# The low parts of three of seven weight operands: from a VectorE subtraction to a ScalarE copy and an accumulating DMA

## The chip, the cores and the metric

The kernel runs on one core of one Trainium2 chip. The metric is the device time of one execution in microseconds. TensorE multiplies, VectorE (DVE) and ScalarE (ACT) do elementwise work, GpSimd (POOL) does some sums, masks and reductions, and SyncE (SP) issues nearly all DMAs. Each engine runs its own instructions in order; semaphores tie them together.

## The reference

Two layers over 1024 tokens of 1024 features, in float32. Layer 0 mixes by forgetting attention (8 heads of 128), layer 1 by chunkwise retention (4 heads, keys of 256, values of 512, chunks of 64). Each mixer is followed by a SwiGLU block of inner width 2816. Every block reads an RMS-normed input and adds its result to the residual stream; a last RMS norm ends it.

```python
def swiglu(h, w_in, w_out):
    gu = h @ w_in
    return (jax.nn.silu(gu[..., :D_FF]) * gu[..., D_FF:]) @ w_out

for i in range(DEPTH):
    h = rmsnorm(x, norm_mix[i])
    j = i // N_MIXERS
    if i % N_MIXERS == 0:
        x = x + forgetting_attention(h, fox_w_in[j], fox_b_f[j], fox_w_out[j])
    else:
        x = x + retention(h, ret_w_in[j], ret_w_out[j])
    h = rmsnorm(x, norm_ffn[i])
    x = x + swiglu(h, ffn_w_in[i], ffn_w_out[i])
return rmsnorm(x, final_norm)
```

## The kernel before

**Products in three passes.** TensorE multiplies float32r operands, which keep fewer bits than float32. Each operand is therefore held as the sum of a high part, the operand rounded to float32r, and a low part, the rest. A product takes three matmuls: high by high, high by low, low by high. `split` (line 97) makes the two parts: a ScalarE copy rounds (line 98), a VectorE subtraction makes the rest (line 99). A weight's parts are called wh and wl, an activation's parts b.

**Seven products for eight.** From the attention's output on, most weight products go by a Strassen-Winograd scheme. A pair of column tiles is cut into four blocks of 128 x 512: A11, A12, A21, A22. Seven weight operands are made of them: A11, A12 and A22 are blocks as they come from memory; S1, S2, S3 and S4 are sums and differences that VectorE makes (lines 588, 589, 606, 611). `Blocks` loads a pair as two tiles `st` of 512 KB through SP (line 577) and splits each operand on demand (`get`). `Products` runs one operand through 12 matmuls of 128x512: for four feature tiles, lines 638 (wh by high), 639 (wh by low) and 640 (wl by high). So a pair takes 84 matmuls. `pair_T` uses it for SwiGLU inputs and the retention's queries, keys and gates; `pair_acc` for the pairs of the SwiGLU outputs; `pair_N` does the same by tokens for the retention's values. There are 84 such pairs of blocks: 44 of SwiGLU inputs, 16 of SwiGLU outputs, 16 of queries, keys and gates, 8 of values.

**Buffers.** The parts of weights come from the pool `wp`: six buffers for wh and six for wl. The seventh operand can be split only when the first has left TensorE. The copy of p (line 699) has to take A11's product out of its bank before A12's is added to it.

**What sets the order.** The kernel is written in program order; a scheduler of the framework then puts each engine's instructions in the order they keep on the chip, so operands of neighbouring pairs interleave on TensorE. The order is fixed when the program is built.

**Early operands.** The first pair of three phases has A11 and S2 split ahead of time by `early`, with the plain split.

Of the kernel before, what the change touches and what calls it, by code (L numbers as in the profile page):

```python
# [12 lines left out]
AF = mybir.ActivationFunctionType  # L13
ALU = mybir.AluOpType
# [23 lines left out]
def trunk(ctx, tc, nc, d, out):  # L38
# [22 lines left out]

# [1 line left out]
    bpa = ctx.enter_context(tc.tile_pool(name="bpa", bufs=32))  # L63
    wp = ctx.enter_context(tc.tile_pool(name="wp", bufs=6))
    mp = ctx.enter_context(tc.tile_pool(name="mp", bufs=1, space=PSUM))
    banks = [0]
# [44 lines left out]

# [1 line left out]
    class Norm:  # L113
# [69 lines left out]

    # =================== forgetting attention ===================
    with ExitStack() as fs:
# [11 lines left out]
        norm = Norm(0, fp, "acc", "mx")  # L197
# [217 lines left out]
        reloads = []  # L415
        # the keys of the first two heads, a pass over the features as they come
        ks, pss = [], {}
# [27 lines left out]
        for h in range(FOX_HEADS):  # L445
            if h > 0:
                kk, qq = k1 if h == 1 else k_head(h), q_head(h)
                if h % 2 == 0:
                    vs, _ = v_pair(h // 2, rc)
            if h == FOX_HEADS - 2:  # L450
                os_ = [reload(i) for i in range(FOX_HEADS - 2)]
            if h == FOX_HEADS - 1:
# [1 line left out]
                wo, ops = [], {}  # L454
                for n, b in TILES[:3]:
                    if b == 0:
                        wo.append(wtile(d["fox_o"][n][:, :7 * P], 7))
                    ops[n, b] = mm_fox()
                    mm_u(ops[n, b], wo[n][:6], os_, b, last=False)
            attend(h, kk, qq, vs, dk, rks)  # L460
        os_ += last_o

        # the tiles so far with all heads but the last; the first of them leave the banks
        part = {}
# [15 lines left out]

    # =================== Strassen-Winograd products ===================
    # C = A B with A = W^T in 2 x 2 blocks (two column tiles, even and odd k tiles) and
    # B in 2 x 2 blocks (even and odd k tiles, two token halves): seven products.
    bpb = ctx.enter_context(tc.tile_pool(name="bpb", bufs=24))
# [10 lines left out]

    # where the sums of a phase are kept
    NAMES = ("B11", "T2", "T1", "T3", "B21", "B22", "T4")
# [40 lines left out]
    class Stored:  # L538
        """The sums of a group of four pairs of feature tiles, kept in memory, split at their first use."""

# [23 lines left out]
    def wsplit(src):  # L564
        hi, lo = wh_wl()
        split(hi, lo, src)
        return hi, lo

    class Blocks:
        """The four blocks of a pair of column tiles and their sums, split on demand."""  # L570

        def __init__(self, src):
            self.s1, self.ready = None, {}
            sts = []
            for i in range(2):
                st = sp.tile([P, 1024], F32, tag="st", name=nm("st"), bufs=5)
                nc.sync.dma_start(st, src[:, i * 1024:(i + 1) * 1024])
                sts.append(st)
            self.a11, self.a12 = sts[0][:, 0:512], sts[0][:, 512:1024]
            self.a21, self.a22 = sts[1][:, 0:512], sts[1][:, 512:1024]  # L580
# [15 lines left out]
        def get(self, n):  # L596
            if n in self.ready:
                return self.ready[n]
            if n == "A11":
                return wsplit(self.a11)  # L600
            if n == "S2":
                return wsplit(self.s2)
            if n == "S1":
                return wsplit(self.s1)
            if n == "S3":
                nc.vector.tensor_tensor(self.a21, self.a11, self.a21, op=ALU.subtract)
                return wsplit(self.a21)
            if n == "A12":
                return wsplit(self.a12)
            if n == "S4":  # L610
                nc.vector.tensor_tensor(self.s2, self.a12, self.s2, op=ALU.subtract)
                return wsplit(self.s2)
            return wsplit(self.a22)

# [3 lines left out]
    class Products:  # L618
        """The seven products of one pair of 128-column tiles, feature-major."""

# [21 lines left out]
    def pair_acc(src, X, y, first):  # L642
        """Adds the products of one pair to the sums y over the groups of feature tiles."""
        prod = Products(src, X)
        banks = prod.banks
        if first:
            y.update({n: yu(n) for n in ("11", "12", "21", "22")}, p=qu("p"))

        def add(n, bk):
            nc.vector.tensor_tensor(y[n], banks[bk], y[n], op=ALU.add)  # L650

        def put(n, bk):
            nc.scalar.copy(y[n], banks[bk]) if first else add(n, bk)  # L653

        prod(0)
        put("p", "a")
        prod(1)
        put("12", "b")
        prod(2)
        prod(3)  # L660
        put("22", "b")
        add("22", "c")
        prod(4)
        put("11", "a")
        prod(5)
        add("12", "c")
        prod(6)
        put("21", "b")

    def paired_out(wsrc, stored, scale_rows, xold):  # L670
        """x + (scaled) act @ W over the groups of eight feature tiles whose sums are in memory."""
        ys = [{} for _ in range(4)]
        out = [[None, None] for _ in range(KT)]
        for g, X in enumerate(stored):
            for n in range(4):
                y = ys[n]
                pair_acc(wsrc[g, n], X, y, g == 0)
                if g < len(stored) - 1:
                    continue
                for q in ("12", "21", "22"):  # L680
                    nc.vector.tensor_tensor(y[q], y[q], y["p"], op=ALU.add)
                for i in range(2):
                    for h in range(2):
                        u = y[f"{i + 1}{h + 1}"]
                        if scale_rows:
                            nc.vector.tensor_tensor(u, u, R[:, HALF[h]], op=ALU.mult)
                        xo = sp.tile([P, H], F32, tag="xo", name=nm("xo"), bufs=2)
                        nc.sync.dma_start(xo, xold[2 * n + i][:, HALF[h]])
                        nc.vector.tensor_tensor(u, u, xo, op=ALU.add)
                        out[2 * n + i][h] = u  # L690
        return out

    def pair_T(src, X):
        """Feature-major C11, C12, C21, C22 of one pair of 128-column tiles."""
        prod = Products(src, X)
# [20 lines left out]
    def pair_N(srcs, X):  # L716
        """Token-major C11, C12, C21, C22 of one pair of 256-column tiles, as two tiles of two token blocks."""
        ws = [Blocks(s) for s in srcs]
# [58 lines left out]
    def load_units(pool, src, gate=None):  # L777
        """A feature tile over all tokens from memory, split in two, by token halves."""
        r = []
# [10 lines left out]
    def out_proj(wsrc, y, acts, xnew, gi, nextw, pools):  # L790
        """y + act @ W: returns the operands of the next phase and its norm."""
        norm = Norm(gi, sp, "sc", "sacc", 4)
# [17 lines left out]

    # =================== SwiGLU ===================
    def ffn(i, X, nrm, xold, xnew, last, nw, pools):
# [60 lines left out]

# [1 line left out]
    norm = Norm(1, sp, "sc", "sacc", 4)  # L875
# [34 lines left out]

    # =================== retention ===================
    qd = [[dp.tile([P, S], F32, tag=f"qd{k}", name=f"qd{k}") for k in range(2 * h, 2 * h + 2)] for h in range(RET_HEADS)]
# [81 lines left out]
    def load_k(h):  # L994
        """Keys by feature, split, and the first half of them times kappa by token, split."""
        ks, kf = [], []
# [23 lines left out]
    def state(kt, vv):  # L1020
        """Sum over the first half of the tokens of key times value, by key feature."""
        r = []
# [14 lines left out]
    heads = {}  # L1037
# [131 lines left out]
def _alt(w, i):  # L1169
    """Every other column tile."""  # L1170
    k, n = w.shape
    return w.reshape(k, n // 256, 2, P)[:, :, i].reshape(k, n // 2)


def _quad(u, v, js):
    """A pair of column tiles as four blocks: the first over even and over odd k tiles, then the second."""
    r = [w.reshape(KT // 2, 2, P, -1)[list(js)].transpose(2, 1, 0, 3).reshape(P, 2, -1) for w in (u, v)]
    return np.ascontiguousarray(np.concatenate(r, axis=1).reshape(P, -1))
# [75 lines left out]
```

## Time and profile before

| | |
|---|---|
| time, median of 3 runs | 2627.21 us (2626.6 to 2629.64) |
| span of the profiled execution | 2626.0 us |
| TensorE, matmuls | 2600.0 us, 99%, 12808 instructions |
| VectorE | 1960.2 us, 75% |
| ScalarE | 1155.9 us, 44% |
| POOL | 167.6 us, 6% |
| DMA | 312.11 MB, mean 119 GB/s |

The profiled execution's own time is its span, 2626.0 us; the fastest of the three runs is 0.6 us above it. Matmuls overlap: one lasts about 0.39 us and the next starts 0.23 us after it, so TensorE's time in a stretch is read from how many matmuls start there. Rows of line 638 to 640 are the seven products, rows of 106 to 108 plain products, rows of 737 to 739 the products by tokens.

In time order the program is: the attention to about 500 us, inputs of the first SwiGLU to about 900, its output to about 1165, the retention's projections to about 1610, the retention and its output to about 1960, the second SwiGLU to the end.

### The profile page before, as it was taken

The page shows a single profiled execution, that of the slowest core. Times are in us where ns is not written, and L with a number is a line of the kernel's source. Part 1 is how long each engine was busy: PE and PEld are TensorE (multiplying, and loading weights), DVE is VectorE, ACT ScalarE, POOL GpSimd, SP SyncE. Part 2 cuts the span into 40 slices and gives each one's busy share as a digit, 9 for nine tenths or more (in the row PEclk, how much of TensorE's full clock was granted, in tenths as well). Part 3 has the DMA queues.
Part 4 walks back from the last instruction along what each step waited for, and adds up shares of the span by engine and source line. Part 5 has one row for each costly group of instructions (what it writes and reads, how often), then busy time and mean ns, then how long its engine had stood idle before and what let it go on. Part 6 is the DMA issues. An engine that isn't in the chain of part 4 may idle for free.

```text
span 2626.0 us, 35148 instructions
## 1 busy us (share of the span) xinstructions
PE 2600.0 (99%) x12808; PEld 2179.9 (83%) x12808; DVE 1960.2 (75%) x3367; ACT 1155.9 (44%) x2168; POOL 167.6 (6%) x147
## 2 busy tenths in 40 slices
PE   9999999999999999999999999999999999999998
PEld 8878887888888878889898989898888888887888
DVE  6798888877767778987667676885567776768795
ACT  6566666533233444453333425662353233335533
POOL 0143322000000000001000010000000000000000
PEclk9999999999999999999999999999999999999999
DMA  3111143332332345533332325655522332325441
GB/s 129 44 57 65 49 145 119 122 106 95 109 104 97 109 152 180 167 107 117 104 113 96 113 101 160 189 196 192 190 85 85 104 111 86 109 84 183 156 158 65
DMA packets 137694, 312.11 MB, mean 119 GB/s; under 512 B 15665, under 2 KB 28721, under 8 KB 137521
## 3 DMA queue, kind: packets, MB, share of 16 engines
q1 hardware_dynamic: 136800, 309.33, 35.1%
q8 instruction: 100, 1.64, 0.3%
q14 instruction: 74, 0.60, 0.1%
q10 hardware_dynamic: 720, 0.55, 0.1%
HBM read 217.54 MB, written 92.27 MB: 118 GB/s over the span
## 4 chain that ended last, share of the span: by engine, by line
PE 89%; DMA 4%; DVE 3%; issue 2%; ACT 1%; POOL 0%; SPq 0%; DVEq 0%; POOLq 0%; ACTq 0%
PE mm L638 17%; PE mm L640 17%; PE mm L639 17%; PE mm L106 7%; PE mm L107 7%; PE mm L108 7%; PE mm L738 2%; PE mm L739 2%; PE mm L737 2%; DMA st<-vd 1%; DMA st<-ac_T 1%; PE mm L256 1%; PE mm L258 1%; PE mm L257 1%; DVE b L99 1%
## 5 line engine op out<-in xcount | busy, mean ns | idle before, releaser
L639 PE MATMUL mm<-b,wh 128*128 128x512 f32 x2128 | 836.8, 394 | 0.0
L638 PE MATMUL mm<-b,wh 128*128 128x512 f32 x2128 | 832.9, 395 | 3.2 <-ACT 22_4397_22190 L653 1.8
L640 PE MATMUL mm<-b,wl 128*128 128x512 f32 x2128 | 819.5, 394 | 0.1
L98 ACT CAST wh<-st 128x512 fp32r<-128x512 f32 (+1 forms) x449 | 275.2, 616 | 578.4 <-PE mm L639 409.4
L638 PEld LDWEIGHTS mm<-b,wh 128*128 128x128 f32 x2128 | 400.3, 188 | 97.8 <-ACT 22_4397_22190 L653 2.2
L640 PEld LDWEIGHTS mm<-b,wl 128*128 128x128 f32 x2128 | 399.8, 188 | 94.1 <-DVE wl L99 0.9
L639 PEld LDWEIGHTS mm<-b,wh 128*128 128x128 f32 x2128 | 400.0, 188 | 91.9 <-DVE b L99 0.2
L99 DVE TENSOR_TENSOR wl<-st,wh 128x512 fp32r<-128x512 f32 (+1 forms) x449 | 311.5, 697 | 55.8 <-ACT wh L98 51.8
L98 ACT CAST wh<-s 128x512 fp32r<-128x512 f32 x252 | 156.0, 621 | 413.3 <-PE mm L639 356.8
L106 PE MATMUL mm<-b,wh 128*128 128x512 f32 x736 | 289.7, 397 | 8.4 <-ACT b L126 5.7
L107 PE MATMUL mm<-b,wh 128*128 128x512 f32 x736 | 290.0, 395 | 1.4 <-DVE b L99 1.4
L108 PE MATMUL mm<-b,wl 128*128 128x512 f32 x736 | 289.9, 395 | 0.0
L99 DVE TENSOR_TENSOR wl<-s,wh 128x512 fp32r<-128x512 f32 x252 | 182.6, 727 | 41.4 <-ACT wh L98 39.7
L106 PEld LDWEIGHTS mm<-b,wh 128*128 128x128 f32 x736 | 138.9, 189 | 40.5 <-ACT b L126 6.5
L107 PEld LDWEIGHTS mm<-b,wh 128*128 128x128 f32 x736 | 138.8, 189 | 32.0 <-DVE b L99 1.8
L108 PEld LDWEIGHTS mm<-b,wl 128*128 128x128 f32 x736 | 138.7, 188 | 31.5
L98 ACT CAST b<-st 128x512 fp32r<-128x512 f32 (+1 forms) x216 | 125.1, 612 | 81.7 <-DMA st<-ac_T 30.0
L99 DVE TENSOR_TENSOR b<-st,b 128x512 fp32r<-128x512 f32 (+1 forms) x216 | 140.0, 674 | 27.9 <-ACT b L98 22.5
L711 DVE TENSOR_TENSOR u<-mm,u 128x512 f32<-128x512 f32 x60 | 41.4, 689 | 116.1 <-PE mm L640 115.9
L738 PE MATMUL mm<-wl,b 128*128 128x256 f32 x448 | 126.0, 281 | 0.0
L739 PE MATMUL mm<-wh,b 128*128 128x256 f32 x448 | 125.9, 281 | 0.0
L737 PE MATMUL mm<-wh,b 128*128 128x256 f32 x448 | 125.8, 281 | 0.0
(514 smaller groups left out, 3965.2 us busy)
## 6 DMA issues: line engine op xcount, KB each, us to landing
st<-ffn_in SPq DMA_DIRECT2D x88, 512.0 KB, 3.5
st<-ffn_out_pairs SPq DMA_DIRECT2D x32, 512.0 KB, 5.4
st<-ac_T SPq DMA_DIRECT2D x32, 512.0 KB, 4.6
ac_T<-t SPq DMA_DIRECT2D x48, 256.0 KB, 2.4
st<-ac_B SPq DMA_DIRECT2D x24, 512.0 KB, 4.6
st<-fox_qk SPq DMA_DIRECT2D x32, 256.0 KB, 2.7
xo<-xd SPq DMA_DIRECT2D x32, 256.0 KB, 3.1
ac_B<-p SPq DMA_DIRECT2D x32, 256.0 KB, 3.1
```

The costliest lines, as they stand in the source:

```text
L98: nc.scalar.copy(hi, src)
L99: return nc.vector.tensor_tensor(lo, src, hi.bitcast(F32), op=ALU.subtract)
L106: nc.tensor.matmul(ps, wh, xh, start=(first and k == 0), stop=False)
L107: nc.tensor.matmul(ps, wh, xl, start=False, stop=False)
L108: nc.tensor.matmul(ps, wl, xh, start=False, stop=(last and k == n - 1))
L638: nc.tensor.matmul(ps, hi[:, js], th, start=f, stop=False, skip_group_check=not new)
L639: nc.tensor.matmul(ps, hi[:, js], tl, start=False, stop=False, skip_group_check=not new)
L640: nc.tensor.matmul(ps, lo[:, js], th, start=False, stop=(j == 3), skip_group_check=not new)
L711: nc.vector.tensor_tensor(u2, banks["c"], u2, op=ALU.add)
L737: nc.tensor.matmul(o, th[:, tk], hi[:, js], start=f, stop=False, skip_group_check=sk)
L738: nc.tensor.matmul(o, th[:, tk], lo[:, js], start=False, stop=False, skip_group_check=sk)
L739: nc.tensor.matmul(o, tl[:, tk], hi[:, js], start=False, stop=(j == 3), skip_group_check=sk)
```

## The change

For A11, A12 and A22, apart from the early A11s, a new function `wsplit_added` takes the place of `wsplit`. The high part is a ScalarE copy as before. The low part begins as a second ScalarE copy with a scale of -1, which rounds to the same float32r value with the other sign. Then a DMA that POOL issues adds the block, read from memory again, to it. VectorE has no part in it. `Blocks` keeps the source in memory for that. The new lines move later line numbers by 9: lines 638 to 640 become 647 to 649, line 699 becomes 708, lines 820 and 822 become 829 and 831, lines 932 and 933 become 941 and 942.

```diff
+    def wsplit_added(src, mem):
+
+
+        hi, lo = wh_wl()
+        nc.scalar.copy(hi, src)
+        nc.scalar.activation(lo, src, AF.Copy, scale=-1.0)
+        nc.gpsimd.dma_start(lo, mem, accum_op=ALU.add)
+        return hi, lo
+
...
         def __init__(self, src):
-            self.s1, self.ready = None, {}
+            self.s1, self.ready, self.src = None, {}, src
...
             if n == "A11":
-                return wsplit(self.a11)
+                return wsplit_added(self.a11, self.src[:, 0:512])
...
             if n == "A12":
-                return wsplit(self.a12)
+                return wsplit_added(self.a12, self.src[:, 512:1024])
...
-            return wsplit(self.a22)
+            return wsplit_added(self.a22, self.src[:, 1536:2048])
```

**ScalarE at an A12 of the retention's keys, before.** The first row is the cast of A12's high part, the second the copy of p, then come two SiLUs of the gates and the casts of S4 and A22. The low part is a row of VectorE.

```order
L98 CAST wh_12194<-st_12110 128x512
L699 COPY p_2451_12131<-mm_12118 128x512
L960 ACTIVATE u_2438_12043<-u_2438_12043 128x512
L960 ACTIVATE c_2439_12045<-c_2439_12045 128x512
L98 CAST wh_12211<-s_2453_12134 128x512
L98 CAST wh_12228<-st_12112 128x512
```

The same place now:

```order
L573 CAST wh_12301<-st_12216 128x512
L708 COPY p_2451_12238<-mm_12225 128x512
L574 ACTIVATE wl_12302<-st_12216 128x512
L969 ACTIVATE u_2438_12147<-u_2438_12147 128x512
L969 ACTIVATE c_2439_12149<-c_2439_12149 128x512
L98 CAST wh_12319<-s_2453_12241 128x512
L573 CAST wh_12336<-st_12218 128x512
L574 ACTIVATE wl_12337<-st_12218 128x512
```

The second copy, wl_12302, stands behind the copy of p.

**TensorE at the same A12, now.** The last matmul that reads the S4 operand before it (wh_12169, wl_12170), whose buffers this A12 takes over, has 18 rows between it and the first row of this A12, the third below.

```order
L648 MATMUL mm_12267<-b_10965,wh_12263 128x512
L649 MATMUL mm_12267<-b_10964,wl_12264 128x512
L647 MATMUL mm_12225<-b_10974,wh_12301 128x512
L648 MATMUL mm_12225<-b_10975,wh_12301 128x512
L649 MATMUL mm_12225<-b_10974,wl_12302 128x512
L647 MATMUL mm_12225<-b_10978,wh_12301 128x512
```

The third A12 matmul is the first that reads the low part, so 20 matmuls stand between the release of the buffers and it. Before, it was 22: 20 rows stood between the release and A12's first row, since two more matmuls of the pair ahead came in between.

**ScalarE at a pair of the first SwiGLU's inputs, now.** The rows go from S3's cast through A12, S4 and A22 to the next pair's A11.

```order
L98 CAST wh_6511<-st_6448 128x512
L829 ACTIVATE u_1307_6369<-u_1307_6369 128x512
L573 CAST wh_6531<-st_6446 128x512
L98 CAST wh_6549<-s_1325_6471 128x512
L574 ACTIVATE wl_6532<-st_6446 128x512
L573 CAST wh_6566<-st_6448 128x512
L831 ACTIVATE u_1301_6333<-u_1301_6333 128x512
L708 COPY p_1323_6468<-mm_6455 128x512
L574 ACTIVATE wl_6567<-st_6448 128x512
L573 CAST wh_6594<-st_6590 128x512
L574 ACTIVATE wl_6595<-st_6590 128x512
```

Here the second copy of A12 (wl_6532) stands behind the cast of S4 (wh_6549). Before, the same stretch held the casts alone, one to an operand.

**POOL in the retention's projections, now.** The sums of rotated keys and queries (lines 941 and 942) and the accumulating DMAs share POOL's queue.

```order
L942 TENSOR_TENSOR m_2474_12365<-m_2474_12365,c_2464_12299 128x512
L941 TENSOR_TENSOR m_2471_12354<-m_2471_12354,u_2463_12297 128x512
L942 TENSOR_TENSOR m_2472_12355<-m_2472_12355,p_2451_12238 128x512
L575 DMA wl_12611<-ret_qk 128x512
L575 DMA wl_12646<-ret_qk 128x512
L575 DMA wl_12693<-ret_v 128x512
L575 DMA wl_12698<-ret_v 128x512
```

Before, this queue held the sums alone.

## The prediction

> **What bounds the kernel now.** I read the page's busy shares first, then TensorE by stretch, then who waits for whom.
>
> ```profile
> span 2626.0 us, 35148 instructions
> PE 2600.0 (99%) x12808; PEld 2179.9 (83%) x12808; DVE 1960.2 (75%) x3367; ACT 1155.9 (44%) x2168; POOL 167.6 (6%) x147
> ```
>
> TensorE is busy in 2600 of 2626 us. A busy PE need not be a full one, so the stretches come next (columns: PE, PEld, DVE, ACT, POOL busy with their instructions, granted clock, DMA share, GB/s).
>
> ```profile
> 500.00:900.00 400.00, 400.00 (x1741) 325.01 (x1740) 288.40 (x474) 129.43 (x219) 0.00 (x0) 1.00 0.28 95
> 1000.00:1090.00 90.00, 89.84 (x387) 72.29 (x386) 83.21 (x139) 35.35 (x64) 0.00 (x0) 1.00 0.50 162
> 1165.00:1610.00 445.00, 445.00 (x2589) 391.21 (x2587) 312.61 (x478) 161.33 (x351) 50.30 (x32) 1.00 0.33 109
> ```
>
> The first SwiGLU's input products issue 1741 matmuls in 400 us, 0.23 us each, at full clock. Its output pairs (1000:1090) keep that pitch with VectorE at 92% (83.21 of 90). So VectorE is well filled, yet TensorE hardly waits for it:
>
> ```profile
> PE mm L106 <- ACT b L126: 5.7, 2, 5.5
> ...
> PE rw L165 <- DVE rs_d L153: 1.6, 1, 1.6
> PE cs L159 <- DVE acc L139: 1.5, 1, 1.5
> PE mm L107 <- DVE b L99: 1.4, 1, 1.4
> ...
> PE mm L638 <- DVE 12_1832_9061 L650: 0.2, 1, 0.2
> ...
> ACT wh L98 <- PE mm L639: 766.2, 395, 4.6
> ```
>
> Columns: total us, times, longest. In the seven-product code TensorE's one wait for VectorE is 0.2 us. The last row matters more: ScalarE waits for TensorE 395 times, for a weight buffer. Six operands fit the ring, and the split of the next starts when the oldest leaves. What counts is therefore the time from that release to TensorE's first use of the low part.
>
> **What is removed.** 249 low-part subtractions leave VectorE (84 pairs of tiles, three operands each, less three early A11s):
>
> ```profile
> L99 DVE TENSOR_TENSOR wl<-st,wh 128x512 fp32r<-128x512 f32 x433 | 303.4, 704 | 55.7 <-ACT wh L98 51.8 <-PE mm L108 1.6
> L98 ACT CAST wh<-st 128x512 fp32r<-128x512 f32 x433 | 267.8, 620 | 573.5 <-PE mm L639 409.4 <-PE mm L107 77.3 <-issue 33.9
> L822 ACT ACTIVATE u<-u 128x512 f32<-128x512 f32 x44 | 27.8, 633 | 3.1 <-DVE u L821 3.1
> L699 ACT COPY p<-mm 128x512 f32<-128x512 f32 x60 | 34.8, 579 | 0.0
> L932 POOL TENSOR_TENSOR m<-m,u 128x512 f32<-128x512 f32 x8 | 13.9, 1738 | 0.0
> ```
>
> 249 x 0.704 = 175 us of VectorE. In time they are worth what TensorE waits for VectorE: 0.2 us here, 4.7 us with the other three rows, which lie at norms. I take -2 us, ends 0 and -5.
>
> **What is added on ScalarE.** 249 scaled copies, priced by the 633 ns ACTIVATE: 158 us. They fit, since ScalarE has 129 of 400 us busy in the first stretch and TensorE's pitch covers them; their delay to the low part is counted below. Without that cover they would cost 158 us.
>
> **What is added on the queues.** 249 accumulating transfers of 256 KB, issued by POOL after the second copy. Nothing like that is in this trace: the queue list has hardware-issued queues and instruction fetches alone. The nearest rows (KB each, median us from issue to landing):
>
> ```profile
> q1 hardware_dynamic: 136800, 309.33, 35.1%
> q10 hardware_dynamic: 720, 0.55, 0.1%
> st<-fox_v SPq DMA_DIRECT2D x12, 256.0 KB, 2.5
> x<-xT SPq DMA_DIRECT2D x16, 256.0 KB, 5.3
> st<-ret_v SPq DMA_DIRECT2D x16, 512.0 KB, 3.4
> st<-ret_qk SPq DMA_DIRECT2D x16, 512.0 KB, 4.3
> st<-ffn_out_pairs SPq DMA_DIRECT2D x32, 512.0 KB, 5.4
> ```
>
> Call D the time from the end of the second copy until TensorE may use the sum. The low end is the fastest plain 256 KB load, 2.5 us. The high end is the slowest, 5.3, plus POOL's longest simple instruction, 1.7: 7.0. An accumulation has to take in the block and the tile, 512 KB, so the nearest rows are 512 KB loads of ordinary stretches (3.4 and 4.3), plus about 1 us on POOL: **D = 4.75**, also the middle of the ends. The spread of single transfers I take as half the width of the 256 KB rows, 1.4 us either way. The traffic, 65 MB on top of 309 MB that take 35.1%, adds 7% as plain transfers and some 15% with both reads; shares of 28 to 50% leave room, so it costs nothing but D.
>
> A rule of the Trainium skill gives another D: "DMA: Bandwidth & Descriptors", section "Anatomy of one DMA — SWDGE (gpsimd) path", fits a fixed 2 us plus the bytes at 436 GB/s, an estimate of 2.6 us here, or 3.2 with the bytes counted twice. By that the sum below would be near 7 us or 20 us instead of 57. No row of this trace shows such a transfer.
>
> **Where D decides.** From the order I counted the matmuls that stand between the last use of the reused buffer and the first use of the new low part. A22 always has 62 or more. A12 has few:
>
> - 13 to 20 matmuls: 15 places (13; 15 and 17 and 18 twice each; 20 eight times), of them 6 in the output pairs, 7 in the retention's keys, queries and gates, 2 in the SwiGLU inputs;
> - 24 to 29: 9 places (24, 28, three of 27, four of 29);
> - 30 to 37: 46 places, 38 of them in the SwiGLU inputs, and there every second A11 belongs with them (19 places of 62 matmuls, but behind four other ScalarE instructions). With one or two of the A11s that have 38, some 66.
>
> What ScalarE does meanwhile, at one A12 of before (columns: start, us):
>
> ```profile
> 1251.47 0.62 ACT L98 CAST wh<-st 128x512 fp32r<-128x512 f32 x1 [0.92 <-PE mm L639]
> 1252.00 0.58 ACT L699 COPY p<-mm 128x512 f32<-128x512 f32 x1
> 1252.13 0.69 DVE L99 TENSOR_TENSOR wl<-st,wh 128x512 fp32r<-128x512 f32 x1 [1.03 <-ACT wh L98]
> 1254.05 0.40 PE L640 MATMUL mm<-b,wl 128*128 128x512 f32 x1
> 1254.28 0.40 PE L638 MATMUL mm<-b,wh 128*128 128x512 f32 x1
> ```
>
> VectorE ran beside ScalarE's copy of p, and the low part was there 1.35 us after the cast began. Now the second copy stands behind the copy of p: instructions start 0.53 us apart, so it ends 0.53 + 0.53 + 0.63 = 1.7 us after the cast began, and D follows. A matmul ends 0.17 us after the next one starts (0.40 against 0.23), and the weights load 0.19 us ahead:
>
> ```profile
> L640 PEld LDWEIGHTS mm<-b,wl 128*128 128x128 f32 x2128 | 399.8, 188 | 94.1 <-DVE wl L99 0.9
> ```
>
> So n matmuls leave n x 0.23 - 2.1 us for D.
>
> - 15 places: 0.9, 1.35, 1.8, 2.0 and 2.5 us, mean 2.1. Each is short by 4.75 - 2.1: 15 x 2.65 = 40 us.
> - 9 places: mean 4.2, short by 0.55: 5 us.
> - 66 places. An A12 with 32 matmuls leaves 5.3 us. One with 34 waits on ScalarE behind S4's cast, whose buffers come free 7 matmuls later: 7.8 - 1.6 - 0.17 - 1.16 - 0.19 = 4.7. The A11 has 36 matmuls from that release to its low part and five ScalarE instructions: 8.3 - 0.17 - 2.75 - 0.19 = 5.2. Mean 5.05, 0.3 above D; with a spread of 1.4 either way the mean shortfall is 1.1 x 1.1 / (2 x 2.8) = 0.22: 14 us.
>
> A late low part stops TensorE, whose queue is in order; nothing behind it runs, and all later releases slide by as much. Sum: 40 + 5 + 14 - 2 = **+57 us**, 2626 + 57 = 2683; the median of the runs shown, 2627.2, is 1.2 above this span, so **2684**. At D = 2.5 only seven of the 15 are short, by 6 us: +4. At D = 7 it is 74 + 25 + 129 = +228, less 2.
>
> POOL's own queue adds a wait: in the retention a transfer stands behind four sums of rotated keys (up to 1.7 us each, the POOL row above). Those are A12s with 30 matmuls or more; I leave them in the spread. The moved pieces (ten matmuls of the next S2 ahead of the next A11; loads one place apart on SP) are work that was there before: no cost.
>
> **Rivals.**
>
> 1. *The transfer is hidden* (11%, not slower than the resolution). Place: the 15 A12s. If D is 2.4 us or less, the eight with 20 matmuls are in time, the other seven cost 5 us and VectorE's relief takes some back: 2627 to 2630. For it: the 2.5 us row. Against it: every 512 KB row is 3.4 us or more, and POOL comes on top.
> 2. *Relief wins* (5%). VectorE at 92% in the output pairs loses 48 subtractions; if that ends unseen waits, the gain is at most TensorE's time not busy, 26 us, of which the waits named for VectorE are 5: 2617 to 2621. Against it: only 0.2 us of these lies there.
> 3. *POOL is held up* (13%). If preparing the transfer waits for VectorE, busy 72 to 92% in 0.7 us pieces, three such waits put D at 7: 2626 + 226 + 1 = 2853. It decides from D = 5.05 on, where the 66 places begin to pay in full, 66 us for each further us. For it: VectorE is rarely idle. Against it: no row shows POOL held up by VectorE.
>
> The skill's "SBUF — State Buffer", "Who interferes with whom", has the rule behind the third: two-port VectorE operations shut GpSimd out while it writes descriptors, tensor_tensor is inferred not to. The rows here that are moved or stay are nearly all TENSOR_TENSOR, so by that rule D stays small; no run here shows it yet.
>
> **How the numbers follow.** Forecast, D between 2.7 and 6.3: 71%; its own range, 2634 to 2800. A run of this kernel tells a difference from about 0.2%, 5 us. Faster is rival 2, 5%; within 0.2% is rival 1, 11%, and one point of the forecast's low edge; slower is the rest, 83%. The range 2632 to 2820 leaves out rivals 1 and 2 and the upper part of rival 3.
>
> **What would show it.** TensorE waits named on the low part's DMA, at matmuls of line 649 after A12, total 50 to 70 us, most in the output pairs and the retention, 0 to 1 us per two pairs in the SwiGLU inputs; VectorE busy near 1785 us, ScalarE near 1315; a POOL queue of 249 x 256 KB with 3.5 to 5 us to landing. If landing is under 2.5 us, or no such waits show, the forecast is wrong; if the SwiGLU inputs' 1741 matmuls need over 415 us, D was above 6.

## The result, and the profile after

The changed kernel takes 2663.32 us (median of 4 runs, 2662.98 to 2665.26) beside 2628.43 us (2626.6 to 2629.92) for the kernel before on the same chip: a ratio of 1.0139, 95% interval 1.0126 to 1.0152. It is 35 us slower. The prediction said 57 us slower, so the side was right, the time was inside the range, and the loss was forecast 22 us too large. The runs below show that its parts were off by more than that, in both directions.

From the page of the changed kernel: span, busy shares, and the DMA queues (packets, MB, share of 16 engines' span).

```profile
span 2660.8 us, 35809 instructions
PE 2611.7 (98%) x12808; PEld 2185.3 (82%) x12808; DVE 1819.6 (68%) x3118; ACT 1282.2 (48%) x2417; POOL 384.3 (14%) x396
...
q1 hardware_dynamic: 136800, 309.33, 35.7%
q0 software_dynamic: 35856, 65.29, 14.6%
```

VectorE lost 141 us of work and ScalarE gained 126. The new queue q0 takes 14.6% for 65 MB, where the plain queue takes 35.7% for 309 MB: 1.9 times as much for each MB.

TensorE's waits in the changed kernel (total us, times, longest):

```profile
PE mm L649 <- DMA wl<-ffn_out_pairs: 17.8, 11, 2.8
...
PE mm L647 <- DVE 22_1738_8851 L659: 2.2, 1, 2.2
PE mm L647 <- DVE 22_4397_22415 L659: 1.8, 1, 1.8
...
PE mm L649 <- DMA wl<-ffn_in: 0.8, 2, 0.6
```

The new waits on transfers lie in the output pairs. In the SwiGLU inputs they are less than a microsecond, in the retention no more than one or two.

The same 12,512 matmuls can be paired in the two traces, and the start of each compared. By that, TensorE falls behind by 17 us in the first SwiGLU's output pairs and by another 17 us in the second's. Over everything between them it loses 2 us, over the first SwiGLU's inputs nothing. Two stretches of the SwiGLU inputs and the retention's projections, and two of output pairs, after (the columns are those of the prediction's stretches):

```profile
500.00:900.00 400.00, 399.40 (x1737) 324.36 (x1737) 253.35 (x412) 160.68 (x279) 52.96 (x61) 1.00 0.54 135
1165.00:1610.00 445.00, 442.99 (x2547) 387.50 (x2546) 279.33 (x425) 193.75 (x410) 109.03 (x100) 1.00 0.58 146
900.00:940.00 40.00, 36.37 (x150) 28.80 (x149) 31.03 (x50) 26.95 (x50) 4.49 (x6) 0.96 0.84 246
2480.00:2520.00 40.00, 35.05 (x137) 27.09 (x136) 29.76 (x49) 23.03 (x44) 4.36 (x5) 0.91 0.79 234
```

The two stretches of output pairs before:

```profile
900.00:940.00 40.00, 39.13 (x169) 31.38 (x168) 35.90 (x60) 24.60 (x45) 0.00 (x0) 1.00 0.76 248
2480.00:2520.00 40.00, 40.00 (x173) 32.00 (x172) 38.35 (x64) 9.75 (x17) 0.00 (x0) 1.00 0.41 135
```

Where before 169 and 173 matmuls start in 40 us, it is 150 and 137 now, and the granted clock is below 1.00, which it never was there before. What that is, the timeline of TensorE shows at the first wait on a transfer (start, us; in brackets the idle time before it):

```profile
931.11 0.40 PE L648 MATMUL mm<-b,wh 128*128 128x512 f32 x1
934.32 0.79 PE L649 MATMUL mm<-b,wl 128*128 128x512 f32 x1 [2.81 <-DMA wl<-ffn_out_pairs]
934.91 0.63 PE L647 MATMUL mm<-b,wh 128*128 128x512 f32 x1
935.34 0.63 PE L648 MATMUL mm<-b,wh 128*128 128x512 f32 x1
...
937.82 0.39 PE L648 MATMUL mm<-b,wh 128*128 128x512 f32 x1
```

After 2.81 us of idleness matmuls start every 0.43 us, and 3.4 us later every 0.23 us again. The record of the granted clock in this trace has seven such periods at half clock in mid-run, each 3.41 us long, all in the output pairs; the trace of before has none. Each holds eight matmuls in place of some fifteen, so it costs about 1.6 us. **The sum of the loss:** 17.8 us on transfers, 4.0 on VectorE's additions of a bank (line 659), 7 x 1.6 = 11 at half clock: 33 of the 34.8 us by which the two spans differ.

### The profile page after: what moved, and what is told of

Same layout as the page of the kernel before. It is cut to its first block, busy times and chain, and to the rows that moved or that the text cites. A ratio compares the mean times of both kernels' runs of the same rounds, so it can differ in the third digit from the quotient of the medians.

```text
span 2660.8 us, 35809 instructions
## 1 busy us (share of the span) xinstructions
PE 2611.7 (98%) x12808; PEld 2185.3 (82%) x12808; DVE 1819.6 (68%) x3118; ACT 1282.2 (48%) x2417; POOL 384.3 (14%) x396
## 3 DMA queue, kind: packets, MB, share of 16 engines
q1 hardware_dynamic: 136800, 309.33, 35.7%
q0 software_dynamic: 35856, 65.29, 14.6%
## 4 chain that ended last, share of the span: by engine, by line
PE 85%; issue 6%; DMA 5%; DVE 2%; ACT 1%; POOL 1%; SPq 0%; POOLq 0%; DVEq 0%; ACTq 0%
PE mm L649 16%; PE mm L647 16%; PE mm L648 16%; PE mm L106 7%; PE mm L107 7%; PE mm L108 7%; DMA wl<-ffn_out_pairs 3%; PE mm L747 2%; PE mm L748 2%; PE mm L746 2%; PE mm L256 1%; PE mm L258 1%; PE mm L257 1%; DMA st<-vd 1%; DMA wl<-ffn_in 1%
## 5 line engine op out<-in xcount | busy, mean ns | idle before, releaser
L649 PE MATMUL mm<-b,wl 128*128 128x512 f32 x2128 | 825.8, 397 | 19.2 <-DMA wl<-ffn_out_pairs 17.8
L573 ACT CAST wh<-st 128x512 fp32r<-128x512 f32 x249 | 153.9, 618 | 264.7 <-PE mm L648 239.5
L575 POOL DMA_DIRECT2D wl<-ffn_in x130 | 113.4, 872 | 1134.0 <-ACT wl L574 888.0
L98 ACT CAST wh<-st 128x512 fp32r<-128x512 f32 (+2 forms) x200 | 121.6, 610 | 253.6 <-PE mm L648 138.7
L99 DVE TENSOR_TENSOR wl<-st,wh 128x512 fp32r<-128x512 f32 (+2 forms) x200 | 142.9, 719 | 43.8 <-ACT wh L98 43.0
L597 DVE TENSOR_TENSOR s<-st 128x512 f32<-128x512 f32 x84 | 58.1, 692 | 167.3 <-DMA st<-ffn_in 74.6
L574 ACT ACTIVATE wl<-st 128x512 fp32r<-128x512 f32 x249 | 156.7, 629 | 17.9 <-PE mm L747 17.9
```

The lines of the kernel that those rows point to most:

```text
L98: nc.scalar.copy(hi, src)
L99: return nc.vector.tensor_tensor(lo, src, hi.bitcast(F32), op=ALU.subtract)
L573: nc.scalar.copy(hi, src)
L574: nc.scalar.activation(lo, src, AF.Copy, scale=-1.0)
L575: nc.gpsimd.dma_start(lo, mem, accum_op=ALU.add)
L597: nc.vector.tensor_tensor(self.s1, self.a21, self.a22, op=ALU.add)
```

## The experiments

All twelve are compared with runs of the kernel before on the same chip. For some, TensorE's lag behind the kernel before is given by place, from paired matmuls as above (us, in the profiled executions; "between" is the retention with the second SwiGLU's inputs):

| kernel | first output pairs | between | second output pairs |
|---|---|---|---|
| the change | 17.2 | 2.4 | 16.6 |
| only the output pairs changed | 12.5 | -1.7 | 16.1 |
| all but the output pairs changed | 3.7 | 2.9 | 1.9 |
| transfer overwrites | 10.3 | -0.4 | 11.7 |
| transfer of 64 columns | 8.8 | 1.2 | 11.5 |
| no transfer | -0.1 | 0.9 | 0.6 |
| traffic alone, output pairs | 0.4 | -1.1 | -1.0 |

### Which operands cost

Output pairs back to the plain split, the other 201 operands changed:

```diff
-        def __init__(self, src):
+        def __init__(self, src, added=True):
+            self.part = (lambda t, m: wsplit_added(t, m)) if added else (lambda t, m: wsplit(t))
...
-        prod = Products(src, X)
+        prod = Products(Blocks(src, False), X)
```

> The output pairs of both SwiGLUs (48 of the 249 operands) go back to the VectorE subtraction, the other 201 keep the copy and the accumulating transfer. Theory (late landing in the output pairs alone): the loss of 35 us goes, 2624 to 2631 us, no TensorE waits on a low part's transfer over 1 us in total, and no half-clock stretch. Rival 1 (the transfers' traffic slows everything): most of the traffic is still there, so at least half of the loss stays, 2645 or more. Rival 2 (relief of VectorE is worth something once nothing is late): 2615 to 2622.

Measured: 2631.51 us beside 2625.08, ratio 1.0027 [1.0016, 1.0038]: 6.4 us. That is just above the theory's 2624 to 2631. The waits on transfers that are left come to 1.3 us, none of them in the output pairs. But four waits for ScalarE's casts take 5.9 us, nearly all where the output pairs begin, and half clock follows two of them, which the theory had excluded:

```profile
PE mm L648 <- ACT wh L98: 5.9, 4, 3.1
```

So 201 accumulating transfers, with 201 subtractions less on VectorE, are worth neither a gain nor much of a loss.

The reverse, the 48 operands of the output pairs alone:

```diff
+        def __init__(self, src, added=False):
...
+        prod = Products(Blocks(src, True), X)
```

> The reverse: only the 48 operands of the output pairs use the copy and the accumulating transfer, 201 go back to VectorE. Theory: the whole loss stays with a fifth of the transfers, 2655 to 2668 us, and 10 or more TensorE waits on them of 15 to 25 us in all. Rival 1 (traffic): the loss shrinks with the traffic to about 7 us, 2632 to 2640.

Measured: 2653.5 us beside 2625.08, 1.0109 [1.0093, 1.0124]: 28.4 us, a little below the theory's range and far above the rival's. With the 6.4 of the other half it makes 34.8, the whole loss. Its waits:

```profile
PE mm L650 <- DMA wl<-ffn_out_pairs: 11.1, 6, 2.3
...
PE mm L648 <- ACT 22_4397_22214 L663: 4.5, 1, 4.5
PE mm L648 <- DVE 22_4397_22214 L660: 2.7, 1, 2.7
```

Transfers are less than half of it, and less than the 15 to 25 us that the theory had.

Only A22, the operand with the most matmuls ahead of it by my count:

```diff
             if n == "A11":
-                return wsplit_added(self.a11, self.src[:, 0:512])
+                return wsplit(self.a11)
...
             if n == "A12":
-                return wsplit_added(self.a12, self.src[:, 512:1024])
+                return wsplit(self.a12)
```

> Only A22 goes by the second copy and the transfer, A11 and A12 by VectorE as before (about 84 transfers in place of 249). Theory (lateness against the time that an operand has; A22 has 62 matmuls or more): no TensorE wait on transfers, in the output pairs a third of the ScalarE copies and of the traffic, 0 to +10 us: 2625 to 2636 us. Rival (each transfer costs its share whatever the operand): a third of the loss, +12 us, with waits on A22's transfers. Second rival (with its lateness covered, VectorE's relief shows): 5 us or more under before.

Measured: 2641.94 us beside 2625.82, 1.0062 [1.0047, 1.0077], 16 us, above the theory's 0 to 10. The waits for it are again in the output pairs, on transfers and, longer, on a cast of ScalarE:

```profile
PE mm L647 <- ACT wh L98: 5.4, 3, 4.1
PE mm L649 <- DMA wl<-ffn_out_pairs: 4.6, 3, 2.7
```

So in the output pairs A22 is late too, although, by the buffers' addresses in this program, the three operands that TensorE waited for had 47 or 48 matmuls ahead of them. Their second copies ended some 5 us after the buffers came free: something beside the transfers costs time there. The next runs look for that.

### The traffic

All operands split on VectorE as before, and for each also the accumulating transfer, into one spare tile that nobody reads:

```diff
+        split(hi, lo, src)
+        nc.gpsimd.dma_start(spare, mem, accum_op=ALU.add)
```

> All splits by VectorE as before, and beside each of the 249 splits POOL issues the same accumulating transfer of the block into one spare tile that nobody reads. Theory: nobody waits for it, so 2625 to 2634 us, though plain loads land later than before. Rival 1 (traffic): 2645 to 2665.

Measured: 3043.46 us beside 2625.08, 1.1588 [1.1572, 1.1605]. The run doesn't measure what it was meant for: transfers into one tile wait for each other, and POOL's queue is in order, so the sums of rotated keys (line 943) stood behind them, and in the retention's projections TensorE waited 390 us at one place:

```profile
PE mm L749 <- DVE wl L99: 390.0, 1, 390.0
```

The same in the output pairs alone, where POOL has nothing else to do and transfers lie further apart:

> All operands are split on VectorE as before; in the output pairs alone each A11, A12 and A22 also sends its accumulating transfer, into one spare tile that nobody reads (48 transfers of 256 KB). TensorE can't wait for these. Theory (in the output pairs the traffic itself delays the loads of weights and stored sums, on which ScalarE and VectorE wait and behind them TensorE): both output stages lose 7 to 12 us each with half-clock periods, 2640 to 2650 us. Rival (the traffic is free, the loss comes from lateness of the low parts and from ScalarE's extra copies): within 0.2% of before, 2621 to 2631 us.

Measured: 2626.09 us beside 2626.46, ratio 0.9999 [0.999, 1.0008]. The transfers were made (issues: KB each, median us to landing), and no time went:

```profile
spare<-ffn_out_pairs POOLq DMA_DIRECT2D x48, 256.0 KB, 4.3
```

My theory for this run, that the traffic itself delays the loads of the output pairs, falls; the rival holds. ScalarE's order in this kernel is that of the kernel before but for 9 of 2112 rows, a point that matters below.

### The lateness, and what isn't lateness

The transfer overwrites the low part with the block and adds nothing, so the low parts are whole blocks; TensorE's, ScalarE's, VectorE's and SP's orders are those of the change, row by row:

```diff
-        nc.gpsimd.dma_start(lo, mem, accum_op=ALU.add)
+        nc.gpsimd.dma_start(lo, mem)
```

> As the change, but the transfer overwrites the low part with the block and adds nothing (the accumulation is left out, so the low parts are not what they should be). The order on TensorE is that of the change. Theory (late landing): a plain transfer of 256 KB from POOL lands 1.5 to 2.5 us earlier than the 5.4 to 6.5 us of the accumulating one, and most of the loss goes: 2628 to 2642 us. Rival 2 (the scheduler's new order of TensorE is what costs): the order is the same, so 2655 to 2665. Rival 3 (POOL's issue is slow, not the accumulation): landing stays above 5 us and so does the time.

Measured: 2647.81 us beside 2625.08, 1.0083 [1.007, 1.0097], between the theory's range and the second rival's. A plain transfer lands sooner in the SwiGLUs (4.0 and 4.2 us against 5.4 and 6.2; POOL is at each 0.53 us against 0.87), and TensorE hardly waits for it:

```profile
wl<-ffn_in POOLq DMA_DIRECT2D x130, 256.0 KB, 4.0
...
wl<-ffn_out_pairs POOLq DMA_DIRECT2D x48, 256.0 KB, 4.2
```

Yet 23 us are lost:

```profile
PE mm L647 <- ACT wh L573: 6.8, 4, 3.1
...
PE mm L647 <- DVE 22_4397_22415 L659: 3.4, 1, 3.4
PE mm L647 <- DVE 22_1738_8851 L659: 2.7, 1, 2.7
...
PE mm L649 <- DMA wl<-ffn_out_pairs: 1.5, 3, 0.8
```

With the same order on every engine, accumulating in place of overwriting is thus 12 of the 35 us. An eighth of the bytes, accumulated, tells whether the transfer's size makes the rest:

```diff
-        nc.gpsimd.dma_start(lo, mem, accum_op=ALU.add)
+        nc.gpsimd.dma_start(lo[:, 0:64], mem[:, 0:64], accum_op=ALU.add)
```

> The change with a transfer of 64 of the 512 columns (the other columns of the low parts stay the negated high part). As many transfers, each an eighth of the bytes. Theory (size decides, through landing and the DMA engines' work): landing under 3 us, no wait on transfers, as without transfers: 2625 to 2637 us. Rival (ScalarE's extra copies and the changed order of the output pairs cost by themselves, as the overwriting transfer suggests, which nobody waited for): 2640 to 2655 us.

Measured: 2645.2 us beside 2625.85, 1.007 [1.0053, 1.0087], 19 us: the rival, though the landing is 3.5 to 5.3 us and not under 3. There is no wait on a transfer, and the waits for ScalarE's casts are 14.3 us:

```profile
PE mm L647 <- ACT wh L98: 7.7, 3, 4.2
PE mm L647 <- ACT wh L573: 6.6, 2, 4.0
```

They are four stalls of 2.8, 3.1, 4.1 and 4.4 us (start to start, less the usual 0.23 us), with 24 us at half clock behind them, at the four places where a group of output pairs begins. There SP loads fourteen stored sums (ac_T, ac_B) and the weights of the pairs through one ring of five tiles `st`. The chain of waits of this kernel ahead of the third stall:

```profile
2397.98 5.45 DMA st<-ac_B
...
2403.51 1.14 ACT b L98 x2
2404.65 0.52 ACT wh L573
2405.18 0.54 ACT wl L574
...
2405.73 7.52 DMA st<-ffn_out_pairs
...
2413.33 0.63 ACT wh L573
```

A stored sum lands, ScalarE casts it, then comes to the second copy of a pair's operand, which gives the tile back; the load of the next pair starts then, takes 7.5 us, and only after it comes the cast for which TensorE waits. Before, the first load of the pairs goes out here:

```profile
2394.98 3.95 SPq L577 DMA_DIRECT2D st<-ffn_out_pairs  x3
```

TensorE is 8.7 us behind by then; with that taken off, the load goes out at 2397.0, 2 us later than before, at a place where before has a stall of 2 us already. Which instruction gives tiles back has changed everywhere. SP's longest wait by far, before:

```profile
SPq L577 <- DVE wl L99: 701.9, 131, 13.5
```

and after:

```profile
SPq L586 <- ACT wl L574: 595.1, 102, 10.6
```

VectorE's subtraction was the last reader of a loaded block, and now it is ScalarE's second copy, in a queue that itself waits for loads.

The copies without any transfer:

```diff
-        nc.gpsimd.dma_start(lo, mem, accum_op=ALU.add)
```

> The transfer is left out, so the low parts of the 249 operands are the negated high parts and the products are not those of the reference; the second ScalarE copies stay, VectorE's 249 subtractions stay away, POOL's queue is as before. Theory (what costs is the lateness of the transfer and, in the output pairs, ScalarE's extra copies in front of other casts): no wait on transfers, SwiGLU inputs and retention at no loss, the output pairs at +5 to +20 us from waits for ScalarE and VectorE with half-clock periods behind them, 2631 to 2645 us. Rival (ScalarE's copies are free, everything comes from the DMA): within 0.2% of before, 2622 to 2630 us. Second rival (VectorE's relief is worth something once the DMA is gone): under 2620 us.

Measured: 2632.55 us (2629.22 to 2638.34) beside 2625.82, 1.0034 [1.0019, 1.0048]: 6.7 us, inside the theory's range. The profiled execution is the fastest of the five, 3.4 us above the median of before; it shows no more than 2.5 us of waits for a first copy and no loss in the output pairs, where the theory had put it. So the second copies alone don't make the 19 to 23 us. But the framework orders this program anew: with the second copies left out of the count, 81 of ScalarE's 2112 rows stand in another place than in the change, against 32 with 64 columns. And VectorE, relieved of 249 subtractions, gives nothing back.

To test the return of the tiles by itself, the second copy reads the high part, which holds the same value, so that the tile is free after the first copy:

```diff
-        nc.scalar.activation(lo, src, AF.Copy, scale=-1.0)
+        nc.scalar.activation(lo, hi, AF.Copy, scale=-1.0)
```

> The change, but the second ScalarE copy reads the high part instead of the loaded tile (the same value with the other sign), so that the tile is not held until the second copy; transfers unchanged. Theory (in the output pairs the second copies, in order behind casts of stored sums, give the five loaded tiles back late, and so all later loads come late): 10 us or more of the change's 35 come back, 2632 to 2650 us. Rival (the late transfer alone stops TensorE, and the tiles are held by other readers anyway): as the change, 2655 to 2670 us.

Measured: 2662.62 us beside 2625.85, 1.0142 [1.0127, 1.0157]: as the change, so the theory's 10 us didn't come. By place, the output pairs lost 14 and 14 us where the change loses 17 and 17, and the waits for line 659 fell from 4.0 to 2.0 us. The waits on transfers stayed at 17.7 us, and the rebuilt order added one in the retention:

```profile
PE mm L649 <- DMA wl<-ffn_out_pairs: 17.7, 9, 3.0
...
PE mm L649 <- DMA wl<-ret_qk: 5.0, 1, 5.0
```

The block from the tile on the chip in place of memory:

```diff
-        nc.gpsimd.dma_start(lo, mem, accum_op=ALU.add)
+        nc.gpsimd.dma_start(lo, src, accum_op=ALU.add)
```

> The change, but the transfer takes the block from the tile on the chip that the two copies read, not from memory again. Theory (what makes the transfer late and slow is the accumulation and the work of POOL's queue, not memory): landing within 0.7 us of the change's median of 5.8, waits on transfers in the output pairs 10 to 25 us, 2650 to 2672 us. Rival (reading memory again is what costs): landing at 4.5 us or less, waits on transfers under 5 us, 2628 to 2645 us.

Measured: 2679.93 us beside 2626.46, 1.0191 [1.0169, 1.0213], outside both expectations. The landing is as the rival said, 3.6 us against 5.4 to 6.5, so reading memory is a good 2 us of the lateness:

```profile
wl<-st POOLq DMA_DIRECT2D x249, 256.0 KB, 3.6
```

But now the transfer gives the tile back, and the loads come later still:

```profile
SPq L586 <- DMA wl<-st: 728.2, 130, 16.1
```

```profile
PE mm L647 <- ACT wh L573: 17.6, 4, 6.2
PE mm L649 <- DMA wl<-st: 14.1, 8, 3.3
```

This looks like the return of the tiles made worse, and it costs 22 us in the first output pairs and 26 in the second: the strongest sign that the ring of loads, not only the low part, sets the time there. It is a sign and no proof, since the framework ordered this program anew, too.

### The room in the ring of weights

The change with five weight buffers in place of six, and the kernel before with five as its control:

```diff
-    wp = ctx.enter_context(tc.tile_pool(name="wp", bufs=6))
+    wp = ctx.enter_context(tc.tile_pool(name="wp", bufs=5))
```

> The change with five weight buffers in place of six. Theory (what decides is the time from the release of a buffer to the first use of its low part against the lateness D of the transfer, with about 0.9 us to spare in the SwiGLU inputs): 12 matmuls less, some 2.8 us, for each operand, so the SwiGLU inputs, which lost nothing with six buffers, now stop TensorE on transfers: 1 to 3 us at most of the 249 operands, 150 to 500 us in all, 2800 to 3200 us. Rival (the transfers are well hidden, and only the output pairs' loads and order cost): at most 30 us more than the change, under 2700 us.

> The kernel before with five weight buffers in place of six: the control for the ring of five. Theory (VectorE's split takes 1.4 us from release to low part, so a ring of five still holds): 0 to 30 us over the kernel before. Rival (five buffers are too few for any split): over 100 us, and then the ring of five says nothing on the transfer.

Measured: the change 2795.89 us, 1.0651 [1.0635, 1.0667]; the control 2634.8 us, 1.0037 [1.0023, 1.005], both beside 2625.82. The control's 9 us are within its theory. The change's theory holds in its mechanism, a little below its range (107 us of waits where it had 150 or more): 12 matmuls less for each operand are 2.8 us, and where SwiGLU inputs had two waits of together 0.8 us there are now forty, 1.7 us each:

```profile
PE mm L649 <- DMA wl<-ffn_in: 69.9, 40, 2.6
PE mm L649 <- DMA wl<-ffn_out_pairs: 17.5, 12, 3.2
PE mm L649 <- DMA wl<-ret_qk: 14.2, 8, 5.4
```

With 5.8 us in the retention's values these are 107 of 170 us; of the rest, 85 us at half clock ahead of the span's end, against 24 in the change, make some 40. So with six buffers the tightest transfers of the SwiGLU inputs are hidden with about a microsecond to spare, and with five they are not. The change's own trace agrees: of these 130 transfers a tenth land 1.0 us or less before the matmul that first reads the low part, a quarter 1.4 us or less.

No kernel of these beats the one before; the nearest, the traffic alone, does nothing useful.

## Why the prediction was right or wrong

**The mechanism was right, the number by luck.** Errors cancel in the sum: D was too small, the places where it decides were too many, and two costs were missing. The sign of 50 to 70 us of waits at line 649 failed: there were 19 at that line. A low part that comes late stops TensorE, at line 649, and the loss is decided by D against the time that an operand has. The ring of five shows it best. VectorE's time was worth nothing, as the sum had it (-2 us): the copies without a transfer are no faster than before, and neither is the kernel with the 201 others changed. The traffic cost nothing, as said.

**D was mis-sized.** I took 4.75 us from plain loads. POOL begins 0.4 us after the copy's end, and from there the transfer takes (issues of the changed kernel):

```profile
wl<-ffn_in POOLq DMA_DIRECT2D x130, 256.0 KB, 5.4
...
wl<-ffn_out_pairs POOLq DMA_DIRECT2D x48, 256.0 KB, 6.2
...
wl<-ret_v POOLq DMA_DIRECT2D x24, 256.0 KB, 6.5
```

so D is about 5.8 to 6.9, and the landing lies above the 3.5 to 5 us that were to show it. The Trainium skill, "DMA: Bandwidth & Descriptors", section "Anatomy of one DMA — SWDGE (gpsimd) path", gave 2.6 us by its fit, or 3.2 with the bytes twice; the traces contradict it for a loaded core, 4.0 us and more for the plain transfer and 5.4 and more for the accumulating one. The 20 us that the prediction gave for a D of 3.2 come to about 15 by its own rooms (15 x 1.1 - 2).

**The count of places failed, and hid that.** With D at 6.2 my own counts would give 15 x 4.1 + 9 x 2.0 + 66 x 1.15 = 155 us. The step "From the order I counted the matmuls that stand between the last use of the reused buffer and the first use" took the six buffers to be reused in the order of the operands' numbers. The addresses in the built program say otherwise. The A12 of the retention's keys, of which I counted 20 matmuls, takes over not the buffers of the S4 operand before it, as I wrote when I described the change, but those of an operand that TensorE left 50 matmuls earlier. Of all 249 operands, three have fewer than 30 matmuls, not 24; half have 52 or more. That A12's second copy, its transfer and the first matmul that reads its low part, in the changed kernel:

```profile
1283.58 0.63 ACT L574 ACTIVATE wl<-st 128x512 fp32r<-128x512 f32 x1
```

```profile
1284.62 0.86 POOL L575 DMA_DIRECT2D wl<-ret_qk  x1 [10.75 <-ACT wl L574]
```

```profile
1294.14 0.40 PE L649 MATMUL mm<-b,wl 128*128 128x512 f32 x1
```

From the copy's end to that matmul it is 9.9 us, where I had 2.5. So the terms of the retention and the inputs in the sum, some 40 us, were in truth about 2; of the 0 to 1 us of waits for every two pairs of SwiGLU inputs that I looked for, 0.8 us showed in all 44 pairs together.

**The output pairs were right by place and by size, for half the reason.** I had six short places there, 16 us; the waits on transfers are 17.8. But they come from ScalarE's delay and long landings rather than from few matmuls. Nine of the eleven operands had 39 to 56 matmuls by address; their second copies ended 2.1 to 6.9 us after the buffers came free, against 1.0 us at the median of the SwiGLU inputs, and their transfers landed 5.7 to 9.8 us after the issue. Only the other two had few, 27 and 28. And two terms that I set at zero are as large; they overlap, since half clock is part of the first too:

- "The moved pieces ... are work that was there before: no cost." With transfers that nobody waits for (overwriting, or of 64 columns) the change's order with its second copies costs 19 to 23 us at the heads of the groups. The chain of waits shows tiles given back by the second copy there; which share is the copies and which the order that the framework made for them is open. The copies in another order (no transfer) cost 6.7 us; other rebuilds cost something at the same heads too (6.4 with the 201 others changed, 9 with five buffers and no copies), while the one kernel that kept ScalarE's order cost nothing. The copy from the high part was to separate the two and didn't. An order held fixed while one copy is moved wasn't tried.
- Nothing in the sum was for the clock, which is 11 us of the 35. The Trainium skill, "TensorE: Matmul & The Clock Gate", section "What's actually happening", puts the drop to half clock after an idle window of about 3.4 us. The length of the slow period agrees, 3.41 us; but here stalls of 2 to 3 us were enough.

**The rivals.** Relief brought nothing. The transfer is hidden outside the output pairs, but not by a D of 2.4. POOL wasn't held up by VectorE: an issue took 0.87 us on average, and no more in the stretch 900:940, where VectorE is 78% busy (4.49 us for six). The third rival was wrong in its cause and near in its D.

## What to carry to other kernels

When an operand's last step moves to another engine, three times move with it: when the operand is ready, how far its engine's queue is pushed back, and when the tile it was read from is given back; where one ring of tiles feeds both weights and activations, these runs point to the third as costing as much as the first, though they don't part it from the changed order. Count the room of a ring from the buffers' addresses, not from the order of names, and then test it with one buffer less: a transfer that is hidden with a microsecond to spare looks the same as one hidden by ten. And a stall of TensorE of about 2 us or more is to be priced at its length plus, mostly, some 1.6 us.

## What the runs showed of the hardware beyond that

- **Half clock after short stalls.** In the change, the seven periods of 3.41 us followed TensorE stalls of about 2 to 3 us, one of them two shorter stalls close together. The length of a stall alone doesn't decide: with five buffers, 22 of 28 stalls of 2 us or more were followed by a slow period within 8 us, six of up to 2.7 us were not. Its place counts too: in each trace the changes of the granted clock lie whole multiples of 3.41 us apart, so a stall can fall into one window of that grid or be shared by two. In the traces of the change and of its form with five buffers, TensorE was idle for 1.81 us or more in each of the 32 full-speed windows that had half clock behind them, and for 1.80 us at most in all the others. Over all the traces the two kinds overlap, between 1.5 and 1.9 us. Some periods are twice or three times 3.41 us (6.83, 10.24).
- **What accumulation costs.** At the same size, order and place, an accumulating transfer keeps POOL 0.87 us against 0.53 and lands, in the SwiGLUs, after 5.4 and 6.2 us against 4.0 and 4.2. It takes 14.6% of the DMA engines against 8.4%. An eighth of the bytes lands there in 3.5 and 4.1 us, so most of the time isn't bytes.
- **Reading on the chip.** With the block taken from a tile on the chip the accumulating transfer lands in 3.6 us, 2 us sooner than from memory.
